# Two channel groups turned over on TensorE in the opening of a hybrid decoder block

## Chip, core and metric

The kernel runs on one core of a Trainium2 chip. The metric is device time in microseconds, the median of several executions; less is better. The core's engines are TensorE (PE: matrix products, with its own weight loads PEld), VectorE (DVE), ScalarE (ACT), GpSimd (POOL) and SyncE (SP), which here only asks for transfers. Each engine works through its own queue in order, and engines wait for each other by semaphores.

## What is computed

One residual block on `x` of 1024 positions by 1024 channels, in float32. The lines that matter here are the first ones:

```python
mod = c @ w_ada[l] + b_ada[l]
shift, scale, gate = jnp.split(mod, 3, axis=-1)
h = rmsnorm(x, norm_g[l]) * (1.0 + scale[:, None, :]) + shift[:, None, :]
proj = h @ w_in[l]
```

Each position (row of `x`) is divided by its root mean square over the channels; each channel is then scaled by `norm_g * (1 + scale)` and shifted. `h` is multiplied by a wide matrix whose columns feed sliding-window attention, a gated linear recurrence, and gates; those are projected, merged, projected once more, added to `x` and normalised again. All of that comes after the part that the change touches.

## The kernel before

**Layout.** Products need the channels on the partitions, so `h` is held transposed: eight groups of 128 channels (group 0 to 7 in this document), each 128 partitions by 1024 positions, in two halves of 512 positions. `x_t` in memory is `x` transposed on the host, and `load_xt(kc)` loads a group of it. The natural rows `x` are loaded too, in eight blocks of 128 positions (`load_x0(i)`), but only for their squares.

**Precision.** A float32 operand is split into a high part (rounded) and a low part (the remainder); a product is made of three: high by high, low by high, high by low. For the activations these are `hh` and `hl`, for weights `wh` and `wl`. ScalarE makes the high parts (`cast`, L102 and L104; `high`, L381; L491), VectorE the low parts (`rest`, L108 and L110; `low`, L390).

**The opening.** It works in this order, written out by hand for every engine (`manual_schedule`), so each engine's queue is the program's order:
- squares of the row blocks, summed over the channels: `square` on ScalarE (L261), `square_v` on VectorE (L265), into one column of `rr` per block
- `root_of(hf)` (L364) takes the root for four blocks, that is for one half of the positions; `spread(hf)` inverts it (L368) and spreads it over the partitions by four transposes on TensorE (L370), into a PSUM bank
- `norm(kc)` multiplies a transposed group by that spread factor on VectorE: group 0 in halves out of the bank (L375), the others out of a copy `r_bc` in SBUF (L378)
- `modulate(kc, a)` sums `c * w_ada` for a group's shift (a = 0) or scale (a = 1) on VectorE (L248), out of a tile `wada` loaded by `load_a`; after the scale a small VectorE instruction makes the column `gsc` (L252)
- `high` and `affine` (L381, L385) apply `gsc` and the shift on ScalarE, `low` makes the remainder
- `terms_of` (L419) and `mm_k` (L171) are the products. Four column blocks of the wide matrix are accumulated at once over all eight groups, in the accumulators listed in `starts`: two in `pmain`, one in the banks `bk[2:]`, one in `bk[:2]`.

The loop over groups 1 to 7 that follows (L483 to L526) repeats affine, high part, scaling of the next group, modulation of the next group, low part, products. In its passes for groups 2 and 3 it also splits the second halves of the four weight blocks (`cast_w(i, 1)`, `rest_w(i, 1)`), and in those for 5 to 7 it casts the value weights; both stand behind the next group's modulation in program order.

**Queues and tiles.** All loads here are asked for on SP in program order. `wada` and the row blocks share seven tiles under one tag (`bufs=7`); a load into such a tile waits until its last reader is done. Row block 6 has a tile of its own (`xlast`). Weight halves have six tiles (`r`).

After the opening, later stages are ordered by a planner from costs; the change does not touch it.

Of the kernel before, what the change touches and what calls it, by code (L numbers as in the profile page):

```python
# [17 lines left out]
AF = mybir.ActivationFunctionType  # L18
ALU = mybir.AluOpType
# [3 lines left out]
P = 128  # L23
S = 1024
# [9 lines left out]
PK_C, PK_BSH, PK_BSC, PK_NG, PK_CW, PK_CB, PK_BA, PK_BX, PK_LAM = (  # L34
    0, 8, 16, 24, 32, 64, 72, 80, 88)
# [13 lines left out]
SL = [slice(0, HALF), slice(HALF, S)]  # L49
# [3 lines left out]
def tile_hybrid_block(ctx, tc, x, x_t, pk, rows, posr, posi, c_row, w_ss, w_gate, w_main, w_v,  # L53
                      w_g, w_ap, w_rp, w_out, out):
    nc = tc.nc
    V, A, G, T = nc.vector, nc.scalar, nc.gpsimd, nc.tensor
# [21 lines left out]
    bk = [pb.tile([P, HALF], F32, name=f"bk{i}")[:] for i in range(4)]  # L78
# [5 lines left out]
    ident = const.tile([P, P], F32, name="ident")  # L84
    rbig = const.tile([P, S], BF16, name="rbig")

    def pcol(base, i):
        return pk_t[:, base + i:base + i + 1]
# [56 lines left out]
    hh, hl, whole = [], [], {}  # L145
    for kc in range(KC):
        for lst, nm in ((hh, "hh"), (hl, "hl")):
            if kc < 4:
                a = hba.tile([P, HALF], F32R, name=f"{nm}a{kc}")
                b = b12.tile([P, HALF], F32R, name=f"{nm}b{kc}")  # L150
                lst.append([a[:], b[:]])
            else:
                a = hb.tile([P, S], F32R, name=f"{nm}{kc}")
# [32 lines left out]
    starts = []  # L186
    with ExitStack() as st:
# [19 lines left out]
        xt, wada, halfw = [], {}, {}  # L207

        def load_a(kc, a):
            wa_t = sp.tile([P, D + 1], F32, tag="wada", name="wada", bufs=7)  # L210
            dma(wa_t[:], w_ss[a * D + kc * P:a * D + (kc + 1) * P, :])
            wada[kc, a] = wa_t

        def load_ss(kc):
            for a in range(2):
                load_a(kc, a)

        def load_wh(i, h):
            halfw[i, h] = load_half(w_main[i][:, SL[h]])

        def load_xt(kc):
            dma(xT[kc][:], x_t[kc * P:(kc + 1) * P, :])

        def load_x0(i):
            t = xlast if i == 6 else sp.tile([P, D + 1], F32, tag="wada", name="xt", bufs=7)
            dma(t[:, :D], x[i * P:(i + 1) * P, :])
            xt.append(t[:, :D])

        load_a(0, 0)
        for i in range(4):  # L230
            load_x0(i)
        load_xt(0)
        load_a(0, 1)
        load_wh(0, 0)
        load_x0(4)

        make_identity(nc, ident)
# [8 lines left out]
        def modulate(kc, a):  # L246
            jk = sp.tile([P, D + 1], BF16, tag="junk2", name="jk")
            V.scalar_tensor_tensor(out=jk[:], in0=wada[kc, a][:], scalar=1.0, in1=c_bc[:],  # L248
                                   op0=ALU.mult, op1=ALU.mult,
                                   accum_out=mods[:, a * 8 + kc:a * 8 + kc + 1])  # L250
            if a:
                V.scalar_tensor_tensor(out=gsc[:, kc:kc + 1], in0=mods[:, 8 + kc:9 + kc],  # L252
                                       scalar=1.0, in1=pcol(PK_NG, kc), op0=ALU.add,
                                       op1=ALU.mult)

        def tiny(name, n=64):
            return sp.tile([P, n], F32, name=name)

        def square(i):
            junk = sp.tile([P, D], BF16, tag="junk", name="junk")  # L260
            A.activation(junk[:], xt[i], AF.Square, accum_out=rr[:, i:i + 1])  # L261

        def square_v(i):
            jk = sp.tile([P, D + 1], BF16, tag="junk2", name="jk")
            V.scalar_tensor_tensor(out=jk[:, :D], in0=xt[i], scalar=1.0, in1=xt[i],  # L265
                                   op0=ALU.mult, op1=ALU.mult, accum_out=rr[:, i:i + 1])
# [95 lines left out]
        def root_of(hf):  # L362
            r1 = rr[:, 4 * hf:4 * hf + 4]
            A.activation(r1, r1, AF.Sqrt, scale=1.0 / D, bias=eps[:])  # L364

        def spread(hf):
            r1 = rr[:, 4 * hf:4 * hf + 4]
            V.reciprocal(r1, r1)  # L368
            for j in range(4):
                T.transpose(bk[hf][:, j * P:(j + 1) * P], r1[:, j:j + 1].to_broadcast([P, P]),  # L370
                            ident[:])

        def norm(kc, hf=None):
            if hf is not None:
                V.tensor_tensor(out=xT[0][:, SL[hf]], in0=xT[0][:, SL[hf]], in1=bk[hf],  # L375
                                op=ALU.mult)
            else:
                V.tensor_tensor(out=xT[kc][:], in0=xT[kc][:], in1=r_bc[:], op=ALU.mult)  # L378

        def high(kc, hf):  # L380
            A.activation(hh[kc][hf], xT[kc][:, SL[hf]], AF.Identity,  # L381
                         scale=gsc[:, kc:kc + 1], bias=mods[:, kc:kc + 1])

        def affine(kc, sl=slice(0, S)):
            A.activation(xT[kc][:, sl], xT[kc][:, sl], AF.Identity, scale=gsc[:, kc:kc + 1],  # L385
                         bias=mods[:, kc:kc + 1])

        def low(kc, hfs=(0, 1)):
            for hf in hfs:
# [5 lines left out]
        def cast_w(i, h):  # L395
            W0[i, h] = first[i] if h else slot()
            cast(W0[i, h], halfw[i, h], 0.125 if i > 1 else 1.0)

        def rest_w(i, h):
            rest(W0[i, h], halfw[i, h], 0.125 if i > 1 else 1.0)  # L400
            starts[i][0].append(W0[i, h])
# [10 lines left out]
        def terms_of(kc, hf, accs, terms):  # L412
            for i in accs:
                w, ps = starts[i]
                h_, l_ = w[0]
                cs = slice(kc * P, (kc + 1) * P)
                for ww, xs in ((h_, hh), (l_, hh), (h_, hl)):
                    if (xs is hl) == (terms == "l"):
                        T.matmul(ps[hf], ww[:, cs], xs[kc][hf],  # L419
                                 start=(kc == 0 and ww is h_ and xs is hh), stop=False)  # L420
# [1 line left out]
        some(16)  # L422
        square(0)
        modulate(0, 0)
        for i in (5, 6, 7):
            load_x0(i)
        for i in range(1, 4):
            load_wh(i, 0)
        square(1)
        square(2)  # L430
        some(99)
        load_xt(1)
        load_ss(1)
        square(3)
        modulate(0, 1)
        load_xt(2)
        load_ss(2)
        root_of(0)
        spread(0)
        cast_w(0, 0)  # L440
        norm(0, 0)
        high(0, 0)
        rest_w(0, 0)
        terms_of(0, 0, (0,), "h")
        square(4)
        square_v(5)
        affine(0, SL[0])
        low(0, (0,))
        square(6)
        square_v(7)  # L450
        load_xt(3)
        load_ss(3)
        root_of(1)
        spread(1)
        cast_w(1, 0)
        A.copy(r_bc[:, SL[0]], bk[0])
        rest_w(1, 0)
        A.copy(r_bc[:, SL[1]], bk[1])
        norm(0, 1)
        cast_w(2, 0)  # L460
        high(0, 1)
        rest_w(2, 0)
        affine(0, SL[1])
        cast_w(3, 0)
        norm(1)
        modulate(1, 0)
        rest_w(3, 0)
        low(0, (1,))
        modulate(1, 1)
        terms_of(0, 0, (0,), "l")  # L470
        for i in (1, 2, 3):
            for terms in "hl":
                terms_of(0, 0, (i,), terms)
        terms_of(0, 1, range(4), "h")
        terms_of(0, 1, range(4), "l")
        for i in range(2):
            load_wh(i, 1)
        load_xt(4)
# [1371 lines left out]
```

## Time and profile before

| | |
|---|---|
| median of 3 runs | 932.46 us (929.82 to 933.45) |
| profiled execution | 932.08 us |
| its span, first to last instruction | 929.9 us |
| busy share PE / PEld / DVE / ACT / POOL | 97% / 80% / 73% / 57% / 9% |
| mean granted TensorE clock | 0.998 |

Times in the profile are microseconds from the span's start. In rows of the timeline the first number is the start, the second the duration, then engine, line and operation, output <- inputs, shapes; in square brackets how long the engine had been idle and what released it. In rows of groups the numbers behind the bar are total busy time, mean nanoseconds of one, and idle time before. Instructions of one engine overlap a little: a 128x512 remainder takes 0.69 us and the next starts 0.60 us after it. A matrix product's row is its latency; two of them start 0.23 us apart once the engine runs at its full pace.

### The profile page before, as it was taken

What the parts mean: (1) busy time and instruction counts of PE and PEld (TensorE: products, weight loads), DVE (VectorE), ACT (ScalarE), POOL (GpSimd) and SP (SyncE); (2) the same over time, 40 slices, a digit from 0 to 9 for tenths busy, and PEclk for the clock granted to TensorE, in tenths of its full rate; (3) what the DMA queues carried; (4) which work ended last, traced back from release to release, by engine and by line L of the source; (5) the groups of instructions that cost most, each with busy time, mean ns of one, the idle gap of its engine ahead of it and who ended that gap; (6) DMA issues with size and microseconds to landing.
All of it is one profiled execution on the core that took longest, in us unless ns stands there. A gap on an engine that the chain in (4) does not pass through costs nothing.

```text
span 929.9 us, 12279 instructions
## 1 busy us (share of the span) xinstructions
PE 901.1 (97%) x4217; PEld 745.5 (80%) x4217; DVE 681.1 (73%) x1042; ACT 533.2 (57%) x1026; POOL 85.5 (9%) x146
## 2 busy tenths in 40 slices
PE   3999999999999999999999999999999999999997
PEld 1679888887888888888887887788888888888886
DVE  5986888888769964996677675799999737657422
ACT  5643655454567656775596784788888622213211
POOL 0110000000000000000000001354454300000000
PEclk9999999999999999999999999999999999999999
DMA  9952548862332541444145349897656186536311
GB/s 350 414 187 102 194 152 281 304 232 85 114 110 94 180 161 36 145 164 154 57 141 187 99 173 294 298 335 219 221 178 189 57 317 219 163 123 242 136 68 68
DMA packets 82148, 168.39 MB, mean 181 GB/s; under 512 B 12756, under 2 KB 29140, under 8 KB 82087
## 3 DMA queue, kind: packets, MB, share of 16 engines
q1 hardware_dynamic: 78596, 159.47, 50.0%
q0 software_dynamic: 2192, 6.00, 1.9%
q10 hardware_dynamic: 1298, 2.15, 0.6%
q8 instruction: 33, 0.54, 0.3%
q14 instruction: 29, 0.23, 0.1%
HBM read 118.20 MB, written 49.78 MB: 181 GB/s over the span
## 4 chain that ended last, share of the span: by engine, by line
PE 87%; DVE 7%; DMA 3%; issue 1%; ACT 1%; SPq 0%; POOL 0%; ACTq 0%; DVEq 0%
PE bk L672 43%; PE rp L171 12%; PE pmain L171 6%; PE rp L1713 5%; PE pgate L966 5%; PE pmain L1713 4%; PE bk L171 3%; PE s_ps L1216 2%; PE pv L1288 2%; DVE jk L248 1%; PE pt L1254 1%; DMA wada<-w_ss 1%; DMA ks<-k_d 1%; PE bk L1461 1%; PE bk L1460 1%
## 5 line engine op out<-in xcount | busy, mean ns | idle before, releaser
L672 PE MATMUL bk<-nh,wl 128*128 128x512 f32 x352 | 137.3, 390 | 0.4 <-DVE wl L108 0.4
L672 PE MATMUL bk<-nh,wh 128*128 128x512 f32 x352 | 137.1, 389 | 0.0
L672 PE MATMUL bk<-nl,wh 128*128 128x512 f32 x352 | 137.0, 389 | 0.0
L108 DVE TENSOR_TENSOR wl<-r,wh 128x512 fp32r<-128x512 f32 x109 | 78.6, 727 | 20.3 <-ACT wh L102 20.3
L102 ACT CAST wh<-r 128x512 fp32r<-128x512 f32 x109 | 66.9, 618 | 43.4 <-PE bk L1461 11.6
L672 PEld LDWEIGHTS bk<-nh,wl 128*128 128x128 f32 x352 | 66.1, 188 | 15.1 <-DVE wl L108 1.4
L672 PEld LDWEIGHTS bk<-nh,wh 128*128 128x128 f32 x352 | 66.1, 188 | 13.7
L672 PEld LDWEIGHTS bk<-nl,wh 128*128 128x128 f32 x352 | 66.1, 188 | 13.6
L672 PE MATMUL bk<-hh,wl 128*128 128x512 f32 x176 | 68.6, 390 | 0.0
L672 PE MATMUL bk<-hh,wh 128*128 128x512 f32 x176 | 68.6, 390 | 0.0
L672 PE MATMUL bk<-hl,wh 128*128 128x512 f32 x176 | 68.5, 389 | 0.0
L108 DVE TENSOR_TENSOR wl<-ws,wh 128x512 fp32r<-128x512 f32 x76 | 51.4, 681 | 0.5 <-ACT wh L102 0.5
L1240 ACT ACTIVATE p<-p,small 128x129 f32<-128x129 f32 x128 | 50.1, 402 | 0.0
L102 ACT CAST wh<-ws 128x512 fp32r<-128x512 f32 x76 | 45.8, 614 | 5.4 <-DMA hla<-yl_d 3.7
L60 POOL DMA_DIRECT2D yh_d<-yh x1 | 0.6, 560 | 493.2 <-ACT yh L1033 493.2
L1730 ACT ACTIVATE o<-xo 128x1024 f32<-128x1024 f32 (+2 forms) x10 | 8.9, 889 | 53.2 <-DVE xo L1729 53.2
L672 PEld LDWEIGHTS bk<-hh,wh 128*128 128x128 f32 x176 | 33.0, 188 | 7.6 <-ACT wh L102 0.9
L1216 PE MATMUL s_ps<-ks,qs 128*128 128x256 f32 (+1 forms) x256 | 37.6, 289 | 1.5 <-DVE p L1230 1.4
L672 PEld LDWEIGHTS bk<-hh,wl 128*128 128x128 f32 x176 | 33.0, 188 | 7.0 <-DVE wl L108 0.3
L672 PEld LDWEIGHTS bk<-hl,wh 128*128 128x128 f32 x176 | 33.0, 188 | 6.9
L775 ACT ACTIVATE c<-bk 128x512 f32<-128x512 f32 x29 | 17.3, 598 | 29.9 <-PE bk L672 29.9
L672 PE MATMUL bk<-hha,wl 128*128 128x512 f32 x88 | 34.3, 390 | 0.1
(380 smaller groups left out, 2271.4 us busy)
## 6 DMA issues: line engine op xcount, KB each, us to landing
r<-w_main SPq DMA_DIRECT2D x100, 256.0 KB, 4.2
wada<-w_ss SPq DMA_DIRECT2D x16, 512.5 KB, 8.9
qs<-q_d SPq DMA_DIRECT2D x16, 512.0 KB, 5.8
ks<-k_d SPq DMA_DIRECT2D x24, 192.0 KB, 4.0
xT<-x_t SPq DMA_DIRECT2D x8, 512.0 KB, 9.0
q_d<-rhi SPq DMA_DIRECT2D x16, 256.0 KB, 4.0
q_d<-rlo SPq DMA_DIRECT2D x16, 256.0 KB, 3.9
sma_d<-c SPq DMA_DIRECT2D x16, 256.0 KB, 2.5
```

Source lines behind the costliest of these rows:

```text
L102: A.copy(dst[0][:], src)
L108: V.tensor_tensor(out=dst[1][:], in0=src, in1=f32(dst[0][:]), op=ALU.subtract)
L171: mm = T.matmul(ps[hf], ww, xx[kc][hf], start=(kc == 0 and ww is w_h and xx is xh), stop=(kc == KC - 1 and xx is xl))
L248: V.scalar_tensor_tensor(out=jk[:], in0=wada[kc, a][:], scalar=1.0, in1=c_bc[:], op0=ALU.mult, op1=ALU.mult, accum_out=mods[:, a * 8 + kc: ...
L672: W["pe"] = T.matmul(ps, ww[:, c], b[kc][xx_], start=(first and kc == 0 and i == 0), stop=(kc == 3 and i == 2), skip_group_check=not first)
L775: A.activation(t["t"], s(), AF.Tanh, scale=0.5)
L966: W["pe"] = T.matmul(ps[:, SL[hf]], ww[:, c0:c0 + P], xx_[:, SL[hf]], start=(ic == 0 and i == 0), stop=(ic == 1 and i == 2))
L1216: W["pe"] = T.matmul(o, qs[:, j, qc], ks[:, b, k0 + (0 if n else P):k0 + 256], start=(b == 0), stop=(b == 1))
L1240: A.activation(px[:, j, :], px[:, j, :], AF.Exp, bias=sm[:, 0, j:j + 1], accum_out=sm[:, 1, j:j + 1])
L1254: W["pe"] = T.transpose(pt[:, j, :], px[:, j, 0:P], ident[:])
L1288: W["pe"] = T.matmul(pv[:], b, m[:].rearrange("p j q -> p (j q)"), start=(i == 0), stop=(i == len(prods) - 1))
L1713: T.matmul(ps[:, sl], lhs[k][th][:, ts_], w[:, sl], start=(k == 0 and w is h_ and lhs is mh), stop=(k == KC - 1 and lhs is ml))
```

## The change

Groups 0 and 1 are no longer loaded transposed. Instead the first 256 channels of each natural row block are multiplied by the row's inverse root in place (`scale`, on VectorE for six blocks, on ScalarE for two), and TensorE transposes them into two PSUM banks (`turn`, banks `bk[1]` and `bk[3]`). `high(0, ..)` and `affine(0, ..)` read the bank; group 1 is copied from the bank to SBUF by ScalarE. The spread factor is still made, for groups 2 to 7, and goes to `r_bc` at once.

The four first weight halves are asked for between the rows, ahead of row block 4, and are split before the first high part. Row block 7 and the loads of group 1's modulation are asked for after the first transposes. The square of block 1 moves to VectorE, and so does that of block 6, while that of block 7 moves to ScalarE. The column `gsc` of groups 2 to 7 is made by ScalarE. The first half's products of all four column blocks (terms with `hh`) now stand ahead of the second half's squares.

```diff
         load_a(0, 0)
         for i in range(4):
             load_x0(i)
-        load_xt(0)
         load_a(0, 1)
-        load_wh(0, 0)
+        for i in range(4):
+            load_wh(i, 0)
         load_x0(4)
...
-            if a:
+            if a and kc < 2:
                 V.scalar_tensor_tensor(out=gsc[:, kc:kc + 1], in0=mods[:, 8 + kc:9 + kc],
                                        scalar=1.0, in1=pcol(PK_NG, kc), op0=ALU.add,
                                        op1=ALU.mult)
+            elif a:
+                A.activation(gsc[:, kc:kc + 1], mods[:, 8 + kc:9 + kc], AF.Identity,
+                             scale=pcol(PK_NG, kc), bias=pcol(PK_NG, kc))
...
+        def scale(i, eng):
+            o, r1 = xt[i][:, 0:2 * P], rr[:, i:i + 1]
+            if eng is A:
+                A.activation(o, o, AF.Copy, scale=r1)
+            else:
+                V.tensor_scalar(out=o, in0=o, scalar1=r1, scalar2=None, op0=ALU.mult)
+
+        raw = [bk[1], bk[3]]
+
+        def turn(kc, hf):
             for j in range(4):
-                T.transpose(bk[hf][:, j * P:(j + 1) * P], r1[:, j:j + 1].to_broadcast([P, P]),
-                            ident[:])
...
+                T.transpose(raw[kc][:, j * P:(j + 1) * P],
+                            xt[4 * hf + j][:, kc * P:(kc + 1) * P], ident[:])
...
+        def spread(hf, ps):
+            for j in range(4):
+                T.transpose(ps[:, j * P:(j + 1) * P],
+                            rr[:, 4 * hf + j:4 * hf + j + 1].to_broadcast([P, P]), ident[:])
+            A.copy(r_bc[:, SL[hf]], ps)
...
-        for i in (5, 6, 7):
-            load_x0(i)
-        for i in range(1, 4):
-            load_wh(i, 0)
-        square(1)
+        load_x0(5)
+        load_x0(6)
+        square_v(1)
         square(2)
         some(99)
-        load_xt(1)
-        load_ss(1)
         square(3)
+        root_of(0)
+        invert(0)
+        for i in range(4):
+            scale(i, V)
         modulate(0, 1)
+        for i in range(4):
+            cast_w(i, 0)
+            rest_w(i, 0)
+        turn(0, 0)
+        turn(1, 0)
+        load_x0(7)
+        load_a(1, 0)
+        load_a(1, 1)
         load_xt(2)
         load_ss(2)
...
         high(0, 0)
...
+        spread(0, bk[0])
+        affine(0, 0)
+        A.copy(xT[1][:, SL[0]], raw[1])
+        for i in (0, 1, 2, 3):
+            terms_of(0, 0, (i,), "h")
         square(4)
         square_v(5)
-        affine(0, SL[0])
+        square_v(6)
+        square(7)
+        root_of(1)
         low(0, (0,))
...
+        invert(1)
+        for i in range(4, 8):
+            scale(i, V if i < 6 else A)
+        turn(0, 1)
+        turn(1, 1)
         load_xt(3)
         load_ss(3)
...
+        high(0, 1)
         modulate(1, 0)
...
+        A.copy(xT[1][:, SL[1]], raw[1])
+        affine(0, 1)
+        spread(1, starts[1][1][1])
+        modulate(1, 1)
         low(0, (1,))
...
+        terms_of(0, 0, range(4), "l")
+        terms_of(0, 1, (0, 2, 3, 1), "h")
+        terms_of(0, 1, (0, 2, 3, 1), "l")
```

More of the change, by code (lines that the diff above doesn't have):

```diff
@@ L364, in root_of, with invert, norm, affine @@
             A.activation(r1, r1, AF.Sqrt, scale=1.0 / D, bias=eps[:])
-        def spread(hf):
+        def invert(hf):
             r1 = rr[:, 4 * hf:4 * hf + 4]
             V.reciprocal(r1, r1)
-            for j in range(4):
-                T.transpose(bk[hf][:, j * P:(j + 1) * P], r1[:, j:j + 1].to_broadcast([P, P]),
-                            ident[:])
[L373 to L378, printed above, removed]
+        def scale(i, eng):
[6 more added lines that the diff above has]
+        def turn(kc, hf):
+            for j in range(4):
+                T.transpose(raw[kc][:, j * P:(j + 1) * P],
[5 more added lines that the diff above has]
+            A.copy(r_bc[:, SL[hf]], ps)
+        def norm(kc):
+            V.tensor_tensor(out=xT[kc][:], in0=xT[kc][:], in1=r_bc[:], op=ALU.mult)
         def high(kc, hf):
-            A.activation(hh[kc][hf], xT[kc][:, SL[hf]], AF.Identity,
+            A.activation(hh[kc][hf], xT[kc][:, SL[hf]] if kc else raw[0], AF.Identity,
                          scale=gsc[:, kc:kc + 1], bias=mods[:, kc:kc + 1])
-        def affine(kc, sl=slice(0, S)):
-            A.activation(xT[kc][:, sl], xT[kc][:, sl], AF.Identity, scale=gsc[:, kc:kc + 1],
-                         bias=mods[:, kc:kc + 1])
+        def affine(kc, hf=None):
+            dst = xT[kc][:] if hf is None else xT[kc][:, SL[hf]]
+            A.activation(dst, dst if hf is None else raw[0], AF.Identity,
+                         scale=gsc[:, kc:kc + 1], bias=mods[:, kc:kc + 1])
         def low(kc, hfs=(0, 1)):
@@ L424, in tile_hybrid_block @@
         modulate(0, 0)
-        for i in (5, 6, 7):
-            load_x0(i)
-        for i in range(1, 4):
-            load_wh(i, 0)
-        square(1)
+        load_x0(5)
+        load_x0(6)
+        square_v(1)
         square(2)
         some(99)
-        load_xt(1)
-        load_ss(1)
         square(3)
+        root_of(0)
+        invert(0)
+        for i in range(4):
+            scale(i, V)
         modulate(0, 1)
+        for i in range(4):
[6 more added lines that the diff above has]
+        load_a(1, 1)
         load_xt(2)
         load_ss(2)
[L438 to L441, printed above, removed]
         high(0, 0)
-        rest_w(0, 0)
-        terms_of(0, 0, (0,), "h")
+        spread(0, bk[0])
[3 more added lines that the diff above has]
+            terms_of(0, 0, (i,), "h")
         square(4)
         square_v(5)
-        affine(0, SL[0])
+        square_v(6)
+        square(7)
+        root_of(1)
         low(0, (0,))
-        square(6)
-        square_v(7)
+        invert(1)
[3 more added lines that the diff above has]
+        turn(1, 1)
         load_xt(3)
         load_ss(3)
[L453 to L460, printed above, removed]
         high(0, 1)
[L462 to L465, printed above, removed]
         modulate(1, 0)
-        rest_w(3, 0)
+        A.copy(xT[1][:, SL[1]], raw[1])
+        affine(0, 1)
+        spread(1, starts[1][1][1])
+        modulate(1, 1)
         low(0, (1,))
[L469 to L475, printed above, removed]
+        terms_of(0, 0, range(4), "l")
+        terms_of(0, 1, (0, 2, 3, 1), "h")
+        terms_of(0, 1, (0, 2, 3, 1), "l")
         for i in range(2):
```

## The prediction

> **What bounds the kernel now.** I read the span first, then three stretches of it, then the chain of waits where the opening hands over to TensorE, and last the queues of VectorE and ScalarE.
>
> ```profile
> span 929.9 us, 12279 instructions
> ```
>
> ```profile
> 0.00:28.60 28.60, 11.32 (x24) 5.74 (x25) 18.71 (x55) 16.32 (x28) 0.70 (x6) 1.00 0.93 362
> 28.60:53.46 24.86, 24.16 (x103) 18.61 (x101) 24.53 (x41) 15.95 (x22) 3.22 (x5) 1.00 1.03 412
> 53.46:929.90 876.44, 865.59 (x4092) 721.15 (x4092) 637.91 (x948) 500.95 (x977) 81.59 (x135) 1.00 0.50 169
> ```
>
> The columns are stretch, length, then busy time of PE, weight loads, DVE, ACT and POOL, the granted clock, the DMA share and GB/s. After 53.46 us TensorE is busy 865.59 of 876.44 us, and the change edits nothing there. All that it can move is the moment at which that last stretch begins. Between 28.60 and 53.46 us VectorE is busy 24.53 of 24.86 us: it is as full as TensorE. The chain says which of the two releases the other:
>
> ```profile
> 49.52 1.25 DVE jk L248 x2
> 50.79 0.17 DVE gsc L252
> 50.99 1.26 ACT xT L385
> 52.27 0.63 ACT hh L491
> 52.94 0.50 PE pmain L171
> ```
>
> At 52.94 TensorE begins input channel group 5 (I count the groups of 128 channels from 0), and it begins then because VectorE finished the modulation sums of that group (L248), then the scale column `gsc` (L252), then ScalarE the affine and the high part. **VectorE's queue from about 25 to 51 us is the bound of the opening**, with TensorE close behind it: the first products of group 1 start at 31.34, and between them and 52.94 lie 88 products, 20.0 us at the pitch of the rows of 28.60 and 28.83 below, while 21.6 us passed.
>
> ```profile
> 22.04 1.11 PE L370 MATMUL bk<-ident,rr 128*128 128x128 f32 x4 [3.00 <-DVE rr L368]
> 23.80 0.63 PE L419 MATMUL pmain<-hha,wl 128*128 128x512 f32 x1
> 24.23 0.63 PE L419 MATMUL pmain<-hla,wh 128*128 128x512 f32 x1
> 28.60 0.39 PE L419 MATMUL pmain<-hhb,wh 128*128 128x512 f32 x1
> 28.83 0.40 PE L419 MATMUL pmain<-hhb,wl 128*128 128x512 f32 x1
> 31.34 0.39 PE L419 MATMUL pmain<-hha,wh 128*128 128x512 f32 x1
> ```
>
> So two things must both come earlier: group 5's operand (now 52.9), and the start of group 1 on TensorE (31.34 may slip to 32.9 before it binds).
>
> **The first half of the rows.** The root of rows 0 to 3 needs the natural rows only, and no edit brings those forward:
>
> ```profile
> 11.97 0.30 ACT L364 ACTIVATE rr<-rr,eps 128x4 f32<-128x4 f32 x1
> 13.43 1.23 DVE L248 SCALAR_TENSOR_TENSOR jk<-wada,c_bc 128x1025 bf16<-128x1025 f32 x1 [2.93 <-DMA wada<-w_ss]
> 14.78 0.17 DVE L368 RECIPROCAL rr<-rr 128x4 f32<-128x4 f32 x1
> 16.95 0.81 ACT L381 ACTIVATE hha<-xT,mods,gsc 128x512 fp32r<-128x512 f32 x1 [1.95 <-DVE xT L375]
> ```
>
> The reciprocal now waits behind a modulation in VectorE's queue until 14.78; afterwards it stands ahead and runs at 12.3. Four row scalings follow (12.5 to 13.7), the modulation (13.7 to 15.0), then the four weight remainders, once 15.1. The high part needs `gsc` and the turned rows: about 15.6 instead of 16.95. This is over a microsecond, and worth nothing by itself, since nothing of it is on the chain that ends at 52.94.
>
> **Prices of new operations.** A scaling of 128x256 on VectorE is not in the trace. Nearest rows:
>
> ```profile
> L282 DVE TENSOR_SCALAR r<-trn 128x128 f32<-128x128 f32 x1 | 0.2, 228 | 0.0
> L364 ACT ACTIVATE rr<-rr,eps 128x4 f32<-128x4 f32 x2 | 0.6, 297 | 1.0 <-DVE jk L265 0.9
> L381 ACT ACTIVATE hha<-xT,mods,gsc 128x512 fp32r<-128x512 f32 x2 | 1.6, 816 | 5.2 <-DVE gsc L252 3.3 <-DVE xT L375 2.0
> L102 ACT CAST wh<-r 128x512 fp32r<-128x512 f32 x8 | 4.7, 613 | 2.1 <-DMA r<-w_main 2.1
> L456 ACT COPY r_bc<-bk 128x512 f32<-128x512 f32 x1 | 0.6, 576 | 0.0
> ```
>
> It lies between 0.23 (half as wide, same kind) and 1.22 us (the scaling of 128x1024 at 29.84, quoted below); I take 0.30, beside the same kind. On ScalarE it lies between 0.30 and 0.82; I take 0.45, below the cast of twice the width. A `gsc` column on ScalarE (128x1, two pointer operands) lies between 0.20, which an estimate from the 0.30 of one pointer can't go far below, and 0.82 (two pointers, 512 wide); I take 0.40, near the first. A group of four transposes goes by the group that exists, 1.1 us (the row of 22.04), bounded by half of that when the clock is up. Reading the accumulator bank rather than the scratch memory costs ScalarE nothing visible (0.58 for the copy from a bank, 0.61 for the cast).
>
> **The second half of the rows** carries the chain. Row block 7 decides it. It was asked for at 9.49 and landed 10.1 us later, at 19.6. Now it takes the place of a modulation tile that is read until 15.0, so it is asked for at 15.05.
>
> ```profile
> 9.49 0.33 SPq L60 DMA_DIRECT2D xt<-x  x1
> xt<-x SPq DMA_DIRECT2D x1, 512.0 KB, 10.1
> wada<-w_ss SPq DMA_DIRECT2D x1, 512.5 KB, 4.3
> ```
>
> The first load of this size, asked for into an empty queue, landed in 4.3 us, so 15.05 would permit 19.4. The transfers run one after the other at 412 GB/s (the stretch above), 1.27 us for 512 KB. Ahead of block 7 stand three weight halves more (0.75 MB) and one transposed group less (0.5 MB), a quarter megabyte or 0.6 us: 20.2 us. The later of the two counts, **20.2**, so the 10.1 us were queue and not latency. The modulation loads of group 3 then wait on SP for the transposes of the second half (24.2 us); behind them stand two weight halves and group 4. Landings by then reach to about 28, so a 4.3 us load asked for at 24.2 does not let the queue run dry, and VectorE wants group 3's modulation only at 32. I cost that wait at nothing; without the cover it would be 1.3 us for each load.
>
> Its square, by block 6's:
>
> ```profile
> 19.41 1.04 ACT L261 ACTIVATE junk<-xlast 128x1024 bf16<-128x1024 f32 x1
> 20.36 0.19 ACT L261 ACTIVATION_READ_ACCUMULATOR junk<-xlast 128x1 f32 x1
> ```
>
> From 20.2: square 1.14 (21.35), root 0.31 (21.7), reciprocal 0.2 (21.9), two scalings on ScalarE, 0.9 (22.8; the two on VectorE lie beside them), the last transpose 0.3 (23.1), channel group 1's four 1.1 (24.2), the four that spread the roots 1.1 (25.3). ScalarE meanwhile: high part 23.9, copy of group 1 to 24.8, affine to 25.55, copy of the spread roots to 26.1. VectorE: the two modulations of group 1 from 22.5 to 25.1 with `gsc`, low part 25.6 to 26.2. Then it starts the scaling of group 2 at **26.2**. Its rows of before:
>
> ```profile
> 25.01 1.22 DVE L378 TENSOR_TENSOR xT<-xT,r_bc 128x1024 f32<-128x1024 f32 x1
> 29.84 1.22 DVE L378 TENSOR_TENSOR xT<-xT,r_bc 128x1024 f32<-128x1024 f32 x1
> 38.34 0.08 DVE L248 DVE_READ_ACCUMULATOR jk<-wada,c_bc 128x1 f32 x1
> 38.46 0.16 DVE L252 SCALAR_TENSOR_TENSOR gsc<-mods,pk_t 128x1 f32<-128x1 f32 x1
> 38.54 1.29 DVE L108 TENSOR_TENSOR wl<-r,wh 128x512 fp32r<-128x512 f32 x2
> 44.70 1.29 DVE L110 SCALAR_TENSOR_TENSOR wl<-r,wh 128x512 fp32r<-128x512 f32 x2
> ```
>
> The scaling of group 2 stood at 29.84: **3.6 us gained**. The work removed is group 1's scaling (25.01, 1.14 us until the next) and two halves of group 0's (0.69 each, 1.2 together); the rest is idle time that closes.
>
> **The `gsc` column on ScalarE gives part of it back.** From group 2 on it saves VectorE 0.08 us a group. But ScalarE's queue is in order, and in groups 2 and 3 two weight casts stand behind that column:
>
> ```profile
> 37.65 1.13 ACT L102 CAST wh<-r 128x512 fp32r<-128x512 f32 x2
> 41.00 1.15 ACT L104 ACTIVATE wh<-r 128x512 fp32r<-128x512 f32 x2
> ```
>
> Before, these casts ran at 37.65 and 41.00, ahead of the end of the modulations (38.42 in group 2; as near in group 3), so VectorE's remainders at 38.54 and 44.70 found them done. Now the column waits for the modulation, the casts wait for the column, and VectorE, with nothing else to do in order, waits for the cast: 0.40 + 0.61 + 0.1 of signals instead of the 0.12 from 38.42 to 38.54, **1.0 us lost, twice**. On the path to group 5 the column itself is 0.25 slower (0.47 from the sum to the affine instead of the 0.22 from 50.77 to 50.99).
>
> The sum at group 5's operand: -3.6 - 0.1 + 2.0 + 0.25 = **-1.5**: 51.45 instead of 52.94. For groups 6 and 7 a cast of the value weights now also stands between the column and the affine, 0.6 more. Group 6's operand had 1.0 us to spare (cast at 57.22, first half done at 57.8, wanted at 58.81) and keeps 0.4:
>
> ```profile
> 57.22 1.14 ACT L491 CAST hh<-xT 128x512 fp32r<-128x512 f32 x2
> 58.81 0.62 PE L171 MATMUL pmain<-hh,wh 128*128 128x512 f32 x2
> ```
>
> That TensorE is ready: 16 products are left from 25.3; at 0.23 us group 1 would start at 29.0, at 0.43 us (23.80 and 24.23) at 32.2, and 31.45 is wanted. I take a first half at 0.43 and a second at 0.23: 30.6, which doesn't bind.
>
> [...] In the trace the pitch was still 0.43 at 24.23 and 0.23 at 28.60 though the granted clock shows 1.00 throughout, and TensorE had been at work since the transposes of 22.04. [...]
>
> So 932.08, the profiled execution's own time (2.2 us of it outside its span), becomes 930.6. It lies 0.4 us under the median of the runs shown, 932.46, so the forecast is **931.0**.
>
> **How far the prices can move this case.** Scalings: two on ScalarE are on the path, 0.3 less to 0.75 more. `gsc`: three times on the path, 0.6 less to 1.25 more. Transposes at double pace: 1.0 less. Together -3.4 to +0.5 instead of -1.5: 929.1 to 933.0.
>
> **Rivals.**
> *TensorE's slow clock becomes the bound.* All 16 products at 0.43: group 1 at 32.2, group 5 at 52.2, gain 0.7: 931.7. For it: TensorE would stand idle from the end of the first half's eight products (15.6 + 8 x 0.43 and the wait for the spread roots, about 20) to the transposes from 22. Against it: transposes and products fill 13 to 20 and 22 to 25.3.
> *The gain is swallowed later*, in a wait whose length does not follow TensorE: 932.5. For it: 10.9 us of the last stretch are idle on TensorE. Against it: the longest named wait there is 1.4 us, on VectorE, which follows TensorE:
>
> ```profile
> PE s_ps L1216 <- DVE p L1230: 1.4, 1, 1.4
> ```
>
> *The short prices hold together*: column 0.20, fast transposes, short scalings: 929.1. For it: the bounds; against it: every price must be low.
> *Slower: row block 7 comes late.* It is asked for 5.6 us later than before. If its 10.1 us are latency and not queue, it lands at 25.1, 4.9 later than I have it; group 2's scaling moves to 31.1, 1.3 later than before, and with 2.15 for the column group 5 is 3.4 late: 935.9. It decides from a landing after 21.7. Against it: 4.3 us for the first load.
>
> **How the numbers follow.** Forecast 0.44, slow clock 0.17, swallowed 0.13, short prices 0.14, late block 0.12. A measurement here tells about 0.5% (4.7 us) from no change. Only the far ends of short prices and of the unknown reach faster by that: 0.08. The late block and its worse forms: 0.09 slower. The rest, 0.83, is within it. The range 928.2 to 934.0 takes in all but the late block and half the far ends.
>
> **What will show it.** Group 2's scaling at 26.2 on VectorE, row block 7 landing near 20.2, two waits of VectorE's remainders on ScalarE's casts, about 1 us each, and TensorE starting group 5 near 51.4 on ScalarE's operand. I am wrong if those two waits are missing, if TensorE stands at group 1 later than 31.5, or if the block lands after 21.7.

## The result and the profile after

The median of 20 executions after the change is 928.57 us (926.3 to 930.88), that of 20 before it 931.34 (929.37 to 933.45). The ratio is 0.9972, with a 95% interval of 0.9962 to 0.9981: 2.8 us less, between 1.8 and 3.5. The forecast was 931.0 in a range of 928.2 to 934.0. The three runs of before that the forecast started from had a median of 932.46, 1.1 us above that of all twenty. Of the other 1.3 us of the miss, 1.0 lies in the opening, where 1.5 us were forecast and 2.47 measured; the last 0.3 is less than the interval tells.

The profiled execution took 929.53 us:

```profile
span 927.4 us, 12333 instructions
```

The span is 2.5 us shorter. Where they come from is read off one instruction that both kernels have, the first product with the value weights, which ends the opening. The first fence is the timeline of TensorE before, the second that after (start, duration, engine, line, operation):

```profile
71.50 0.28 PE L1459 MATMUL bk<-wh,hha 128*128 128x256 f32 x1
566.13 1.00 PE L1216 MATMUL s_ps<-ks,qs 128*128 128x128 f32 x8
```

```profile
69.03 0.28 PE L1475 MATMUL bk<-wh,hha 128*128 128x256 f32 x1
563.72 1.00 PE L1232 MATMUL s_ps<-ks,qs 128*128 128x128 f32 x8
```

The opening is 2.47 us shorter. From there to the first attention scores 494.63 us passed before and 494.69 after: nothing is given back. So the whole question lies in the first 70 us.

VectorE's queue after, at the instructions that the prediction named (scaling of groups 2 and 3, then the end of group 3's modulation and the two pairs of weight remainders):

```profile
25.30 1.22 DVE L394 TENSOR_TENSOR xT<-xT,r_bc 128x1024 f32<-128x1024 f32 x1
30.05 1.22 DVE L394 TENSOR_TENSOR xT<-xT,r_bc 128x1024 f32<-128x1024 f32 x1
33.61 0.08 DVE L248 DVE_READ_ACCUMULATOR jk<-wada,c_bc 128x1 f32 x1
34.66 1.30 DVE L108 TENSOR_TENSOR wl<-r,wh 128x512 fp32r<-128x512 f32 x2 [0.97 <-ACT wh L102]
41.69 1.29 DVE L110 SCALAR_TENSOR_TENSOR wl<-r,wh 128x512 fp32r<-128x512 f32 x2 [0.98 <-ACT wh L104]
```

Group 2's scaling stands at 25.30 instead of 29.84, and both forecast waits for ScalarE's casts are there. ScalarE's timeline shows why they arise, and when group 5's operand is cast:

```profile
33.73 0.39 ACT L256 ACTIVATE gsc<-mods,pk_t 128x1 f32<-128x1 f32 x1 [0.30 <-DVE jk L248]
34.02 1.13 ACT L102 CAST wh<-r 128x512 fp32r<-128x512 f32 x2
49.49 1.14 ACT L507 CAST hh<-xT 128x512 fp32r<-128x512 f32 x2
```

The cast stands behind the column, which waits for VectorE's sum. The operand's cast begins at 49.49; it was 52.27.

But that operand no longer releases anything. The chain of waits after, from the request for row block 7 to group 5 (start, length, what):

```profile
14.46 5.12 DMA xt<-x
...
20.85 0.31 ACT rr L367
...
21.85 0.85 PE bk L384 x4
...
22.72 0.78 ACT hhb L397
23.50 0.48 ACT xT L484
23.97 0.68 ACT xT L402
24.65 0.48 ACT r_bc L391
...
25.18 0.80 PE pmain L436
...
51.05 1.81 PE pmain L171 x8
```

After 25.18 the chain is TensorE's own work without a break, through group 5 and beyond. TensorE starts group 5 here, from its timeline:

```profile
25.18 0.80 PE L436 MATMUL pmain<-hla,wh 128*128 128x512 f32 x1 [0.93 <-ACT r_bc L391]
28.34 0.63 PE L436 MATMUL bk<-hhb,wh 128*128 128x512 f32 x1
28.76 0.63 PE L436 MATMUL bk<-hhb,wl 128*128 128x512 f32 x1
30.93 0.40 PE L436 MATMUL pmain<-hha,wh 128*128 128x512 f32 x1
50.89 0.62 PE L171 MATMUL pmain<-hh,wh 128*128 128x512 f32 x2
```

The last row but one is the start of group 1, the last that of group 5: 88 products in 19.96 us, the full pace. The pair at 50.89 takes 0.62, where the pair of before at 52.94 took 1.02 because its second product waited for the operand's other half. Two things hold TensorE up ahead of group 1: it waits 0.93 us for ScalarE's copy of the spread factor, and its products then follow each other at 0.42 us (28.34, 28.76) and not at 0.23. The windows of that stretch, with the granted clock third from the end:

```profile
21.85:25.18 3.33, 2.41 (x13) 1.72 (x13) 3.19 (x7) 2.91 (x7) 0.00 (x0) 0.69 1.01 406
25.18:30.93 5.75, 5.75 (x15) 4.57 (x16) 5.71 (x9) 4.50 (x6) 0.00 (x0) 0.58 1.03 415
```

The clock fell after TensorE had been idle from the last product of the first half to 21.85, as the first of these rows says (the second, the transposes that spread the factor, is used further down):

```profile
21.85 0.55 PE L384 MATMUL bk<-ident,xt 128*128 128x128 f32 x2 [3.63 <-ACT rr L367]
...
22.95 0.88 PE L389 MATMUL pmain<-ident,rr 128*128 128x128 f32 x4
```

So the theory from this trace is: **two chains of nearly the same length** lead out of the opening. One is VectorE's queue, with the two waits that the column on ScalarE causes; the other is TensorE, with the wait for the copy and the low clock. By this theory, taking one shorter gains nothing while the other stands. The rival was that VectorE's queue is still the bound and the two waits cost their 2 us in full.

### The profile page after: what moved, and what is told of

Its sections match the earlier page's. It is cut to its first block, busy times and chain, and to the rows that moved or that the text cites. A ratio compares the mean times of both kernels' runs of the same rounds, so it can differ in the third digit from the quotient of the medians.

```text
span 927.4 us, 12333 instructions
## 1 busy us (share of the span) xinstructions
PE 903.3 (97%) x4233; PEld 749.4 (81%) x4233; DVE 681.1 (73%) x1041; ACT 535.8 (58%) x1034; POOL 84.7 (9%) x146
## 4 chain that ended last, share of the span: by engine, by line
PE 81%; DVE 7%; DMA 7%; issue 2%; ACT 1%; POOL 0%; SPq 0%; ACTq 0%; DVEq 0%
PE bk L688 43%; PE rp L171 9%; PE pgate L982 5%; PE bk L171 4%; PE rp L1729 4%; PE pmain L1729 4%; PE pmain L171 3%; PE s_ps L1232 2%; PE pv L1304 2%; DMA tt<-tr_d 1%; DMA wo<-w_out 1%; PE pt L1270 1%; DMA r<-w_main 1%; PE bk L1477 1%; PE bk L1476 1%
```

## The experiments

In the table "group 1" and "group 5" are the starts of those groups on TensorE, "operand" the start of the cast that makes group 5's, "values" the first product with the value weights, all from each run's timelines. Ratios are against the kernel before on the same chip, with the 95% interval.

| kernel | group 1 | operand | group 5 | values | median us | ratio |
|---|---|---|---|---|---|---|
| before | 31.34 | 52.27 | 52.94 | 71.50 | 931.34 | 1 |
| after | 30.93 | 49.49 | 50.89 | 69.03 | 928.57 | 0.9972 (0.9962 to 0.9981) |
| after, again (r_after) | 29.00 | 49.74 | 50.42 | 68.96 | 927.94 | 0.9965 (0.9953 to 0.9977) |
| e1 column back on VectorE | 30.98 | 47.84 | 50.95 | 69.08 | 927.72 | 0.9955 (0.9942 to 0.9968) |
| e1b, the same again | 31.17 | 47.85 | 51.13 | 69.26 | 927.80 | 0.9952 (0.9936 to 0.9968) |
| e2 order of products | 29.88 | 50.31 | 50.99 | 69.52 | 927.62 | 0.9960 (0.9947 to 0.9972) |
| e3 both | 28.91 | 47.62 | 48.85 | 66.99 | 926.29 | 0.9943 (0.9931 to 0.9956) |
| e3b, the same again | 30.18 | 48.63 | 50.12 | 68.26 | 926.90 | 0.9952 (0.9935 to 0.9969) |
| e4 idle TensorE filled with products | 29.04 | 49.79 | 50.46 | 69.06 | 927.37 | 0.9962 (0.9946 to 0.9977) |
| e5 column, order and filler | 28.65 | 48.12 | 48.79 | 67.36 | 926.74 | 0.9958 (0.9945 to 0.9971) |
| e6 filled with transposes | 28.75 | 49.49 | 50.16 | 68.70 | 928.33 | 0.9974 (0.9964 to 0.9984) |
| e7 weights late | 32.07 | 52.83 | 53.50 | 72.07 | 930.46 | 0.9998 (0.9987 to 1.0008) |
| e8 weights early alone | 33.58 | 53.23 | 53.90 | 72.50 | 932.04 | 1.0013 (1.0001 to 1.0024) |
| e9 casts ahead, order, filler | 28.50 | 47.95 | 48.63 | 67.23 | 927.03 | 0.9945 (0.9928 to 0.9961) |

Apart from e7, the medians of the changed kernels lie within 2.3 us of each other, and their intervals are 1.8 to 3.2 us wide, so the verdicts rest on the traces, and on the medians only for what changes more.

**e1: the column back on VectorE**, which takes away both waits.

```diff
-            if a and kc < 2:
+            if a:
...
-            elif a:
-                A.activation(gsc[:, kc:kc + 1], mods[:, 8 + kc:9 + kc], AF.Identity,
-                             scale=pcol(PK_NG, kc), bias=pcol(PK_NG, kc))
```

> The column gsc of all groups goes back to VectorE; all else is the changed kernel. VectorE theory (the prediction's): VectorE's queue sets the end of the opening, its two waits for casts go (0.97 and 0.98 us in the changed kernel), group 5 starts about 2 us earlier, near 49, and the kernel gains 4.5 to 5 us on the one before. TensorE theory (from the changed kernel's trace): group 1 starts at 30.9 because the 16 products before it begin at 25.2 and run slowly, and from there TensorE never waits; group 5 stays at 50.9 and the gain stays at 2.5 to 2.8 us, though the two waits are gone from VectorE.

The operand's cast on ScalarE and group 5 on TensorE:

```profile
47.84 1.14 ACT L504 CAST hh<-xT 128x512 fp32r<-128x512 f32 x2
```

```profile
50.95 0.62 PE L171 MATMUL pmain<-hh,wh 128*128 128x512 f32 x2
```

The operand is ready 1.65 us earlier than in the changed kernel, and TensorE takes it at 50.95 instead of 50.89. In that execution the column's place makes no difference to the end of the opening, because TensorE is the bound. The rival falls for this trace.

**e2: the order of the first half's low products.** The copy of the spread factor reads the second half of accumulator 1 in `pmain`; the products that wait write the first half of the same tile. Here they come last; by the theory of two chains that brings group 1 forward, and group 5 up to its operand.

```diff
-        terms_of(0, 0, range(4), "l")
+        terms_of(0, 0, (0, 2, 3, 1), "l")
```

> The four low products of the first half go in the order 0, 2, 3, 1, so that the accumulator whose second half holds the spread roots comes last. [...] Group 5 then waits for its operand at 50.1 or starts up to 0.8 us earlier; the kernel gains 0.5 to 0.8 us on the changed one, about 3.3 on the one before. VectorE theory: nothing moves, 2.5 to 2.8 on the one before.

Group 1 starts 1.05 us earlier, at 29.88. Not all of this is the order: the clock, too, came back sooner than in the changed kernel, near 27.7 us instead of 30.0 (worked out at the end). Group 2's scaling came later here (26.14 on VectorE): the second root was 0.37 us later, and the eight transposes before it took 1.76 us instead of 1.1, since the clock was 0.50 for all of 21.85 to 25.18. So in this execution the low clock held up VectorE's chain as well. Now that chain binds:

```profile
44.86 0.49 PE L171 MATMUL pmain<-hh,wh 128*128 128x512 f32 x1 [0.31 <-ACT hh L507]
50.99 1.02 PE L171 MATMUL pmain<-hh,wh 128*128 128x512 f32 x2
```

TensorE waits for ScalarE's operand in group 4, and the pair of 1.02 shows the same in group 5. The opening ends 0.49 later than in the changed kernel (69.52), so the earlier group 1 gained nothing.

**e3: both edits of e1 and e2.**

> Both edits together. TensorE theory: the operand of group 5 comes at about 48, TensorE is ready for it between 49 and 50; the gain on the one before is 3.5 to 4.6 us, more than of either edit alone. VectorE theory: as with gsc on VectorE alone.

```profile
48.85 0.61 PE L171 MATMUL pmain<-hh,wh 128*128 128x512 f32 x2
```

Group 5 begins 2.04 us before that of the changed kernel, and the value products too (66.99 for 69.03). Neither edit alone brought the end of the opening forward; together they shorten both chains. But the execution also had a better clock between 25.18 and 30.93 than e1's (0.87 for 0.59), so part of it may be chance; e3b below is for that.

**e4: filler.** Fourteen products whose result nobody reads stand behind the first half's, to keep TensorE at work until the transposes of the second half.

```diff
             terms_of(0, 0, (i,), "h")
+        for _ in range(14):
+            T.matmul(raw[0], W0[0, 0][0][:, 0:P], hh[0][0], start=True, stop=True)
         square(4)
```

> 14 extra products, whose result nobody reads, stand on TensorE between the first half's products and the second half's transposes, where the changed kernel is idle for 3.55 us (18.30 to 21.85). If that idle stretch is what puts the clock down, the granted clock stays at 1.00, the 16 products run at 0.23 us instead of 0.43, group 1 starts near 29 and group 5 at its operand, 50.1: 0.8 us better than the changed kernel, about 3.3 on the one before. VectorE theory: no gain in time. If the clock falls for another reason, the granted clock dips as before and group 1 stays at 30.9.

```profile
44.33 1.02 PE L171 MATMUL pmain<-hh,wh 128*128 128x512 f32 x2 [0.62 <-ACT hh L509]
```

The granted clock is 1.00 in both stretches, group 1 starts at 29.04, 1.9 us earlier, and TensorE then waits 0.62 for the operand in group 4. The low clock was worth 1.9 us to TensorE's chain, and the 0.8 us expected at the end did not come (69.06), as VectorE's chain was not shortened. The filler even lengthened that chain a little: it ran to 22.4, so the transposes began 0.55 us later and the operand was cast at 49.79 instead of 49.49.

**e5: the edits of e1, e2 and e4 at once.**

> gsc on VectorE, the order 0, 2, 3, 1, and the 14 extra products together. Theory of two chains (VectorE's and TensorE's, 0.8 us apart in the changed kernel): with both shortened the opening ends earlier by more than any edit alone; group 1 at 27 to 27.5, group 5 at its operand near 48; the first value products, at 69.0 in the changed kernel and 67.0 with two of the edits, start between 66 and 67. Gain on the one before 5 to 6 us. Rival, that another thing sets the end behind the opening: no more than the 5.4 us of the two edits, and a start of the value products no earlier than 67.

The value products come at 67.36: 4.1 us before those of the kernel before (the medians differ by 4.0), and the 5 to 6 expected were missed. Group 1 came at 28.65 and not at 27 to 27.5, since the wait for the copy was 0.93 even here. TensorE's timeline says which chain kept it:

```profile
25.57 0.50 PE L433 MATMUL pmain<-hla,wh 128*128 128x512 f32 x1 [0.93 <-ACT r_bc L388]
48.79 1.02 PE L171 MATMUL pmain<-hh,wh 128*128 128x512 f32 x2
```

The pair of 1.02 shows that the operand (its cast begins at 48.12) is the bound again. With both cures of TensorE and the column on VectorE, VectorE's queue is what is left.

**e6: the same gap filled with transposes**, 26 of them, in place of products.

```diff
+        for j in range(26):
+            T.transpose(raw[0][:, j % 4 * P:(j % 4 + 1) * P],
+                        r_bc[:, j % 4 * P:(j % 4 + 1) * P], ident[:])
```

> The changed kernel with 26 extra transposes (into a bank that is overwritten) in place of the 14 extra products. If transposes keep the clock up as products do, the granted clock stays at 1.00 from 18 to 31 us and group 1 starts near 29, as with the products (29.04). If transposes do not count, the clock is down from about 20 at the latest, and group 1 starts at 30 or later, as in the changed kernel (30.93).

```profile
21.85:25.18 3.33, 1.96 (x14) 1.44 (x13) 3.19 (x7) 2.91 (x7) 0.00 (x0) 1.00 1.02 411
25.18:30.93 5.75, 5.73 (x25) 4.75 (x26) 5.71 (x9) 4.51 (x6) 0.00 (x0) 1.00 1.04 415
```

The clock stayed at 1.00 and group 1 started at 28.75. In this gap transposes kept the clock up as the products of e4 did (1.00 in both stretches there too). The time of about 20 in the expectation was my estimate, and no run shows it: in the changed kernel the clock was still 1.00 from 18.30 to 23.10. One trace could be chance, but the mean granted clock of all ten executions of e6 was 0.998 or 0.999, and that of the changed kernel's twenty lay between 0.992 and 0.999. Here the filler delayed nothing: the operand was cast at 49.49 as in the changed kernel, group 5 began at it (50.16), and the opening ended 0.33 us earlier. About so much the low clock cost the end in the changed kernel's trace.

**e7: the weight halves late.** The changed kernel, with three of the four first halves asked for behind row block 6.

```diff
-        for i in range(4):
-            load_wh(i, 0)
+        load_wh(0, 0)
...
         load_x0(6)
+        for i in range(1, 4):
+            load_wh(i, 0)
```

> The changed kernel with the weight halves 1 to 3 asked for behind row block 6 again, not between rows 3 and 4. The casts of these halves stand on ScalarE ahead of the first high part and the square of block 4, so ScalarE is held until the last lands, near 18.5 instead of 14.5: the first high part at 19 instead of 15.1, squares 4 and 7 near 21.5 and 22.7, the second root at 24 instead of 20.9, group 2's scaling 2.5 to 3.5 us later. Expected: the whole gain is lost, -0.5 to +1.5 us against the one before. Rival, that the order of these loads is free because row block 7 decides: group 2's scaling stays at 25.3 and the gain at 2.8.

ScalarE's timeline:

```profile
17.76 0.62 ACT L102 CAST wh<-r 128x512 fp32r<-128x512 f32 x1 [3.77 <-DMA r<-w_main]
...
19.55 0.76 ACT L396 ACTIVATE hha<-bk,mods,gsc 128x512 fp32r<-128x512 f32 x1
...
24.20 0.30 ACT L366 ACTIVATE rr<-rr,eps 128x4 f32<-128x4 f32 x1
```

The casts stand ahead of the first high part, the squares and the second root in ScalarE's queue, so the 3.77 us for the weights make everything behind them late: the second root comes at 24.20 instead of 20.85, the opening ends 3.04 us later than in the changed kernel, and the time is that of before.

**e8: the weight halves early, alone.** The kernel before, with its four first halves asked for where the changed kernel asks.

```diff
-        load_wh(0, 0)
+        for i in range(4):
+            load_wh(i, 0)
         load_x0(4)
...
-        for i in range(1, 4):
-            load_wh(i, 0)
```

> The kernel before with only the order of the four weight halves changed (asked for between rows 3 and 4); groups 0 and 1 are still loaded transposed. Row blocks 4 to 7 land 1.9 us later, block 7 at 21.5 instead of 19.6, its square on VectorE ends near 22.8 instead of 21.4: the second root 1.3 us later, group 5's operand up to 1.3 later. Expected: 0.5 to 1.5 us slower than the one before. Rival, that VectorE's later remainders take less waiting and give it back: no difference.

VectorE's two squares of the second half now wait for their rows:

```profile
18.51 1.23 DVE L266 SCALAR_TENSOR_TENSOR jk<-xt 128x1024 bf16<-128x1024 f32 x1 [1.04 <-DMA xt<-x]
21.09 1.23 DVE L266 SCALAR_TENSOR_TENSOR jk<-xt 128x1024 bf16<-128x1024 f32 x1 [0.74 <-DMA xt<-x]
```

Group 2's scaling moves from 29.84 to 30.79 and the value products from 71.50 to 72.50; the ratio is 1.0013. So early weights alone lose 1.0 us in the opening, turned groups with late weights lose 0.57 there, and both together gain 2.5. That the turned groups need early weights is not shown by this in general: e7 leaves the casts of the weights where the changed kernel has them, ahead of the first high part. A kernel with late weights and late casts was not run.

**r_after, e1b and e3b: the same kernels again**, on one chip, to see how much of e1 and e3 is chance.

> The changed kernel once more, beside the others of this call. Two-chain theory: 2.5 to 2.9 us under the one before, value products from 69.0.

> The kernel with gsc back on VectorE once more, to be read against the changed kernel of this call. Its first measurement was 4.0 us under the one before, while its trace begins the value products at 69.08, no earlier than the changed kernel. Two-chain theory: equal to the changed kernel within 1 us, since TensorE binds in both. VectorE theory, or a gain behind the opening: 1 to 2 us under the changed kernel again.

> gsc on VectorE and the order 0, 2, 3, 1 once more, without extra products. Two-chain theory: value products from 67.0 to 67.5, 1.5 to 2 us under the changed kernel of this call. If its first trace owed its place to the phase in which the clock came up, it stands with the changed kernel, within 1 us.

In r_after the clock did not fall, and the other chain was the bound. Its window, group 1, group 4 and group 5:

```profile
25.18:30.93 5.75, 5.47 (x24) 4.55 (x25) 5.71 (x9) 4.52 (x6) 0.00 (x0) 1.00 1.04 418
```

```profile
29.00 0.39 PE L436 MATMUL pmain<-hha,wh 128*128 128x512 f32 x1
...
44.28 1.02 PE L171 MATMUL pmain<-hh,wh 128*128 128x512 f32 x2 [0.62 <-ACT hh L507]
...
50.42 1.02 PE L171 MATMUL pmain<-hh,wh 128*128 128x512 f32 x2
```

One kernel, two executions, two bounds, and value products at 69.03 and 68.96. This is the clearest sign of two nearly equal chains: the clock moved TensorE's by 1.93 us (29.00 for 30.93) and the end by 0.07. e1b repeats e1 (operand at 47.85, group 5 at 51.13), and its median is that of r_after within 0.2 us. e3b does not repeat e3 in full: its clock was 0.50 and 0.73 in the two stretches, its value products came at 68.26, 0.7 ahead of r_after and not 2.0. So by these two traces the gain of e3 over the changed kernel is between 0.7 and 2.0 us in the opening; in e3b the clock fell early enough to make the eight transposes take 1.76 us, and the second root was 0.56 later (21.29 for 20.73), so group 2's scaling came at 26.20 instead of 25.18.

**e9: the two casts moved ahead of the next group's modulation**, with the column left on ScalarE, and the order and filler of e5.

```diff
+            if kc in (2, 3):
+                for i in (0, 1) if kc == 2 else (2, 3):
+                    cast_w(i, 1)
             if kc + 1 < KC:
...
             if kc in (2, 3):
                 for i in (0, 1) if kc == 2 else (2, 3):
-                    cast_w(i, 1)
                     rest_w(i, 1)
```

> gsc stays on ScalarE, but the casts of the second weight halves are put ahead of it in ScalarE's queue; the order 0, 2, 3, 1 and the 14 extra products as well. Two-chain theory: VectorE's two waits of 1 us go without giving VectorE the column back; value products from 67 to 67.6, equal to the three edits with gsc on VectorE within 0.5 us in the trace; 4 to 5 us under the one before. Rival, that the column's 0.39 us on ScalarE and the casts of the value weights behind it cost as much as they save: 68 or later.

VectorE's remainders:

```profile
34.21 1.29 DVE L108 TENSOR_TENSOR wl<-r,wh 128x512 fp32r<-128x512 f32 x2 [0.29 <-ACT wh L102]
...
40.17 1.29 DVE L110 SCALAR_TENSOR_TENSOR wl<-r,wh 128x512 fp32r<-128x512 f32 x2
```

The waits of 0.97 and 0.98 are 0.29 and none, and the opening ends where e5's does (67.23 for 67.36). The waits came from the casts' place in the queue, as the prediction said, and not from ScalarE's being too slow for the column.

e5 and e9 had the full clock in both stretches, and their openings end 1.6 to 1.8 us before those of the changed kernel's two executions, and the median of e9 is 0.9 us below r_after on the same chip. The intervals of their ratios overlap that of r_after, so a gain over the changed kernel is shown for the opening and not for the whole. (Against the changed kernel's first measurement, 0.9962 to 0.9981, the intervals of e3 and e9 lie wholly lower, but those were not taken side by side.)

**What stays open.** Behind the first scores the profiled executions took between 361.6 and 364.0 us, in kernels whose code behind that point is the same. The changed kernel's two stood at 363.7 and 364.0, e1's two at 362.1 and 361.8. Whether the column's place matters there too, or whether that is chance, these runs don't tell.

## Why the prediction was right and wrong

**Right.**
- The bound of before was VectorE's queue: e8, which made group 2's scaling 0.95 later, made the end of the opening 1.0 later. Group 1 slipped there too, to 33.58, but with 19.96 us of products behind it TensorE would have been ready at 53.54, and it began group 5 at 53.90, 0.67 after the operand's cast began.
- The 10.1 us of row block 7 were queue and not latency: asked for at 14.46, it landed 5.12 later at 19.58 (20.2 forecast from 15.05). The rival with the late block falls. It was asked for 0.6 earlier than I had it, because its place in the tiles is one that the transposes free, not the modulation; SP's waits between 10 and 26 us name them:

```profile
SPq L60 <- PE bk L384: 2.7, 3, 1.5
```

- `gsc` on ScalarE takes 0.39 (0.40 taken), and the two waits are there, 0.97 and 0.98 long (0.40 + 0.61 + 0.1 = 1.11 forecast). A scaling on ScalarE takes 0.51 with the next 0.41 later (0.45 taken).
- The gain is not swallowed: 494.63 and 494.69 us between two marks.

**Wrong: "30.6, which doesn't bind".** The start of group 1 was at 30.93, so the number was nearly right, but by luck. The forecast had 16 products from 25.3, eight of them at the slow pace. In the trace the spreading transposes were done by 23.83, one product ran, the copy held up the other fifteen until 25.18, and eleven of those were slow. What failed is that it was held against 31.45, the start wanted with an operand at 51.45. The operand came earlier than that, so TensorE was wanted earlier too: 49.49 for the cast and 0.67 to the product make 50.16, and 19.96 before that is 30.20. TensorE was 0.73 late, and became the bound in that execution.

**The terms that were mis-sized.** The operand's cast moved by 2.78 us, where 1.5 was forecast:
- Group 2's scaling gained 4.54 and not 3.6. Of the 0.9, the earlier landing of block 7 gives 0.62. From the landing to the second high part it took 3.14 us instead of 2.9, which takes 0.24 back. Group 1's copy was forecast to wait for its transposes and to begin 1.1 behind the high part; the eight transposes of both groups took 1.1 together (21.85 to 22.95), where four had been costed at that, and the copy began 0.78 behind it (22.72 and 23.50 in the chain): 0.32 gained. The copy and the affine then took 1.15 (23.50 to 24.65) instead of 1.35: 0.20 gained.
- Group 2's column, which left VectorE's queue, saved 0.20 and not 0.1: from group 2's scaling to group 3's it is 4.75 us (25.30 to 30.05), where it was 4.95.
- The two waits cost 0.85 and 0.86 net, not 1.0 each: less the 0.12 that the column had taken there, 0.97 and 0.98 were waited and not 1.11. The cast begins 0.29 us after the column's start (33.73, 34.02), not after its full 0.39.
- The column on the path cost 0.23 (0.25 forecast).

-4.54 - 0.20 + 0.85 + 0.86 + 0.23 = -2.80, which is the 2.78 but for rounding. TensorE, as the new bound, let 2.05 of it through at group 5 (50.89 for 52.94), and 0.42 more came from the half-operand wait that group 5 no longer has: 18.14 us from there to the value products instead of 18.56.

**The slow-clock rival** was named with the right cause (TensorE idle for 3.63 us, then a granted clock of 0.69 and 0.58) and the wrong price. It put group 1 at 32.2 with all products at 0.43 us. In the trace the last four of them ran at full pace again (30.02 to 30.93). What I did not see was the wait for the copy, 0.93 us: the spread factor of the second half is made in the other half of the tile that the products go into.

The 931.0 was thus too high by the 1.1 us of its starting point and by these terms; the sign, the range (by 0.4 us at its lower end) and the statement that it lies within 0.5% held. The 0.5% was also taken as what a measurement can tell from no change; twenty executions of each kernel told 0.28%.

## What to carry to other kernels

When a change shortens the chain that binds, work out the margin of the next one against the new time and not the old; here both ended within 0.8 us, and the five runs that mended one of the two alone (e1, e1b, e2, e4, e6) ended the opening at most 0.3 us earlier. In an engine's in-order queue, a small instruction that waits for another engine makes everything behind it wait: 0.4 us of work on ScalarE cost VectorE 0.85, twice, and moving the casts ahead of it cured that. And an early load is only worth what waits for it: early weights alone lost 1.0 us in the opening (e8), and late weights, with their casts left ahead of other work in ScalarE's queue, lost the whole gain (e7).

## What the runs showed of the hardware

**The clock fell behind an idle TensorE, in six of seven executions.** With TensorE idle between the two halves (3.63 us in the changed kernel), the granted clock fell in six of seven profiled executions that have this gap (means of 0.50 to 0.74 over 21.85 to 25.18 in after, e1, e1b, e2, e3, e3b) and stayed at 1.00 in r_after, the same kernel as the first. In the kernel before, TensorE was idle for 3.00 us ahead of its transposes at 22.04, and the clock stayed at 1.00. In e7 the first half's products came later, behind a high part made at 19.55 and not at 15.13, and the clock was 0.75 over 21.85 to 25.18. With the gap filled it was 1.00 in all four (e4, e5, e6, e9).

The low clock in these traces is half of the full one: in e2 and e3b it was 0.50 over all of 21.85 to 25.18, and the pitches of 0.42 and 0.23 fit that. So the means of 0.69 over 3.33 us and 0.58 over 5.75 us in the changed kernel make, as an estimate with these two levels alone, 2.1 and 4.8 us at the low clock: it fell near 23.1 and came back near 30.0, some 6.9 us later, although TensorE was busy for 2.41 us of the first stretch and for all of the second. The same trace gives a mean of 1.00 over 18.30 to 23.10 and 0.51 over 23.10 to 30.00. In e3 the same working (0.71 and 0.87) gives 3.4 us at the low clock, up to 26.7; in e2 (0.50 and 0.78) the clock comes back near 27.7, in e3b (0.50 and 0.73) near 28.3.

The pitch of the products fits these times: it changes from 0.42 to 0.23 us near 30.0 in the changed kernel, and in e2 it is 0.23 from 27.83 on. What sets the times at which the clock falls and comes back, no run tests.

**Transposes kept the clock up.** In e6 transposes alone filled the gap and the clock stayed at 1.00. In the changed kernel too, the products behind twelve transposes stand 0.23 us apart from 16.44 on, though TensorE had been idle for 6.84 us ahead of the transposes:

```profile
12.96 2.07 PE L384 MATMUL bk<-ident,xt 128*128 128x128 f32 x8 [6.84 <-DVE xt L378]
14.82 1.06 PE L389 MATMUL bk<-ident,rr 128*128 128x128 f32 x4
15.94 0.66 PE L436 MATMUL pmain<-hha,wh 128*128 128x512 f32 x1
16.44 0.39 PE L436 MATMUL pmain<-hha,wl 128*128 128x512 f32 x1
16.67 0.40 PE L436 MATMUL pmain<-hha,wh 128*128 128x512 f32 x1
```

These are transposes of float32, which the trace records as plain products (MATMUL); no other kind was run. How soon the full pace comes differs between executions: in e6, behind the same twelve transposes, the products stood 0.43 us apart until 17.88. Nor does the granted clock tell the pace alone: in the kernel before, the products stood 0.43 us apart from 23.37 to 24.65, although the granted clock is given as 1.00 over 22.04 to 25.18.

**A copy out of one half of an accumulator tile held up products into the other half.** The wait on the copy out of `pmain` was 0.93 us in the changed kernel and 1.40 in e6. Ordering those products last started group 1 1.05 us earlier in e2, where the clock differed as well; at the full clock, e9 against e4, it was 0.54 us earlier (28.50 for 29.04), with a wait of 0.93 for 1.39. The trace gives the copy as what released the products, so the program made them wait for it; whether the memory would have made them wait too, the runs don't show.
